# Keeping the first group's rows on the chip, and giving the prefill's operands memory that is released early

## The chip, the cores and the metric

The kernel runs on one core of one Trainium2 chip. The core has five engines with a queue each: TensorE (PE, matrix products), VectorE (DVE), ScalarE (ACT), GpSimd (POOL) and SyncE (SP, which here only issues DMAs). Each works through its instructions in the order of its program. Semaphores make an instruction wait for those of other engines. SBUF is the memory on the chip, PSUM the banks that take PE's results, and DRAM the memory behind the DMA queues. The metric is the time of one execution in microseconds on the device, as the median of several runs.

## What is computed

One layer of a hybrid backbone at width 1024, on 9 blocks of 128 tokens: block 0 is context, blocks 1 to 8 are latent tokens. Cut to what matters here:

```python
mods  = silu(c) @ w_ada + b_ada             # six rows: shift, scale, gate, twice
h     = rmsnorm(x) * (1 + scale1) + shift1
q, k, v, mq, mk, mv, mo, mgates = split(h @ w_in)
a     = attention(q, k, v)                  # 8 query heads, 2 key heads, 512 wide
m     = mlstm_bidir(mq, mk, mv, mgates)     # 4 heads, forward and backward scan, 512 wide
x     = x + gate1 * (concat(a, rmsnorm(m) * sigmoid(mo)) @ w_out)
h2    = rmsnorm(x) * (1 + scale2) + shift2
x     = x + gate2 * (swiglu(h2 @ w_gu) @ w_down)
y     = rmsnorm(x) * final_norm_w
```

The rows that the change is about are `x` after the out-projection, `x + gate1 * (...)`, which are added up in two halves: 512 input columns from attention, 512 from the mLSTM.

## The kernel before

**Tiling.** The 9 blocks form three groups of three (`CB` = 3). Products are made in float32 pieces split in two: a high part (`whi`, `mx`) rounded for PE and a low part (`wlo`, the second half of `mx`), so each product is three matmuls: high by high, high by low, low by high. For a weight piece, SP loads `raw` (128 x 1024 float32, 512 KB), ACT casts it to `whi` (L152), and DVE subtracts to make `wlo` (L137).

**Stages.** Up to about 455 us: norm, input projection, head projections, the scans of the mLSTM heads and the attention of group 0, woven together. Then the scan of the last head, woven with `attn_out_first`, which does the attention half of the out-projection for group 0 alone and leaves its rows in a tile `x1a`. Then `prefill`, about 492 to 560 us, on which the change bears. Then the FFN of the three groups, where PE does products of `aTh`/`aTl` and the gate, up and down weights to the end.

**The prefill.** For each block b = 0 to 8:

- `load_hm(b)`: the mLSTM rows, which the scan has stored to `hm_d` in DRAM, come back as `hmr`.
- `mix(b)`: four transposes on PE (L116), a cast on ACT (L1206) and a subtraction on DVE (L137) make the operand `mx`.
- `half(b, 0)` and `half(b, 1)`: one `out_block` each. It is 12 matmuls (L1163, L1164, L1165) into one of four PSUM banks. Then DVE multiplies by the gate row (L1124) and frees the bank, and POOL adds to the residual rows (L1125).
- for b below 3, `end(b)`: squares and their sum on ACT (L1325, `jk`), a reciprocal root in twelve small DVE steps (L127 to L133), and a block or two later `norm2`: `y` on ACT (L1341), transposes on PE, and the scaled and shifted operands of the FFN.

Blocks 0 and 1 are done together (first halves of both, then second halves), the others one by one. Attention of group 1 is woven in at 0.35 of a step per step: scores S on PE (L1055), their maximum on DVE (L1057), exponential on ACT (L1058, L1061), the low part on DVE (L1062), two DMA transposes (`phT`, `plT`, issued by SP), and the products with the values on PE (L1079, L1080).

The rows of group 0 take a way around: `attn_out_first` keeps `x1a` in memory that is released at its end, so POOL stores the three blocks to `x1a_d` in DRAM (L1297), and SP loads them again as `x` in the prefill (L1185). The second pair of out-projection pieces is issued behind the first two of these loads.

**What sets the order.** The code above is not the order on the engines. A scheduler simulates the program and chooses the next instruction of each engine from those that are ready in its model. Constraints (`issue_after`) and priorities (`hot`) in the code bend its choice. Tile pools decide on memory. A tile that takes the place of another waits until the old one's last reader is done, and a pool opened in place of closed ones inherits their waits. Before, `hmr` and `mx` lie in the pool `xp` on the right side, which takes the place of tiles of the scan that are in use to its end.

The last head's scan is the stage ahead: for each of the three groups POOL multiplies by the output gate (L905), ACT squares (L904, `jkh`), DVE makes the reciprocal root `ry` and POOL multiplies by it (L911). Then the group's rows are stored to `hm_d` (L914, L916): group 0 by SP, group 1 by ACT's queue, group 2 by POOL's queue.

## Time and profile before

| | |
|---|---|
| median of three runs | 1548.04 us (1547.23 to 1548.79) |
| the profiled execution, its own time | 1549.49 us |
| its span, first to last instruction | 1547.7 us |
| mean granted clock of TensorE | 0.981 |
| busy: PE, DVE, ACT, POOL | 1482.8, 1018.6, 772.2, 273.9 us |
| PE busy in 480 to 500, 500 to 510, 520 to 530 us | 13.65 of 20, 8.96 of 10, 3.96 of 10 us |

Busy times of different engines overlap. PE is busy for 96% of the span, so an engine's waits matter where PE waits for it. PE's granted clock is shown as a share of full speed: at 0.5 a matmul takes about twice the time and still counts as busy. The rows of a timeline give the start, the duration, the engine, the line, the operation with its tiles, and in brackets the idle time ahead of it with what ended it.

### The profile page before, as it was taken

What the parts mean: (1) busy time and instruction counts of PE and PEld (TensorE: products, weight loads), DVE (VectorE), ACT (ScalarE), POOL (GpSimd) and SP (SyncE); (2) the same over time, 40 slices, a digit from 0 to 9 for tenths busy, and PEclk for the clock granted to TensorE, in tenths of its full rate; (3) what the DMA queues carried; (4) which work ended last, traced back from release to release, by engine and by line L of the source; (5) the groups of instructions that cost most, each with busy time, mean ns of one, the idle gap of its engine ahead of it and who ended that gap; (6) DMA issues with size and microseconds to landing.
All of it is one profiled execution on the core that took longest, in us unless ns stands there. A gap on an engine that the chain in (4) does not pass through costs nothing.

```text
span 1547.7 us, 23430 instructions
## 1 busy us (share of the span) xinstructions
PE 1482.8 (96%) x8539; PEld 1248.4 (81%) x8539; DVE 1018.6 (66%) x2025; ACT 772.2 (50%) x1429; POOL 273.9 (18%) x356
## 2 busy tenths in 40 slices
PE   6899999999998899999999999999999999999997
PEld 3545567677766679899898989989898989999996
DVE  4878554838657865878646587887866484554554
ACT  4754465947654643555432445556642443323333
POOL 0112422333434352010110101000000101101110
PEclk9899999999998899999999999999999999999998
DMA  9664423522365766878644547878764545544441
GB/s 361 196 193 145 100 70 42 118 52 59 76 217 196 207 136 188 199 155 204 162 137 130 169 138 242 192 171 177 182 145 127 157 151 159 157 133 134 143 144 59
DMA packets 388057, 236.91 MB, mean 153 GB/s; under 512 B 170198, under 2 KB 347686, under 8 KB 387942
## 3 DMA queue, kind: packets, MB, share of 16 engines
q1 hardware_dynamic: 385438, 230.26, 54.4%
q10 hardware_dynamic: 2008, 3.39, 1.0%
q8 instruction: 67, 1.10, 0.3%
q0 software_dynamic: 496, 1.77, 0.3%
q14 instruction: 48, 0.39, 0.1%
HBM read 183.79 MB, written 13.26 MB: 127 GB/s over the span
## 4 chain that ended last, share of the span: by engine, by line
PE 83%; DVE 7%; ACT 4%; DMA 4%; issue 2%; POOL 1%; SPq 0%; ACTq 0%; DVEq 0%
PE mm L1363 12%; PE mm L1364 12%; PE mm L1362 12%; PE mm L1135 5%; PE mm L1136 5%; PE mm L1137 5%; PE S L1055 4%; PE wi L498 3%; PE wi L496 3%; PE wi L497 3%; PE mm L1165 2%; PE mm L1163 2%; PE mm L1164 2%; PE po L1079 2%; PE po L1080 2%
## 5 line engine op out<-in xcount | busy, mean ns | idle before, releaser
L152 ACT CAST whi<-raw 128x1024 fp32r<-128x1024 f32 (+1 forms) x216 | 221.8, 1027 | 395.8 <-PE mm L1363 148.3
L137 DVE TENSOR_TENSOR wlo<-raw,whi 128x1024 fp32r<-128x1024 f32 (+1 forms) x216 | 259.6, 1202 | 178.5 <-ACT whi L152 175.4
L1363 PE MATMUL mm<-aTl,whi 128*128 128x384 f32 x1056 | 355.9, 337 | 2.7 <-DVE aTl L137 2.7
L1364 PE MATMUL mm<-aTh,wlo 128*128 128x384 f32 x1056 | 354.3, 336 | 0.0
L1362 PE MATMUL mm<-aTh,whi 128*128 128x384 f32 x1056 | 353.3, 335 | 0.1
L137 POOL TENSOR_TENSOR hl<-tn,hl 128x384 fp32r<-128x384 f32 x66 | 84.3, 1277 | 846.1 <-ACT hl L1385 730.0
L1363 PEld LDWEIGHTS mm<-aTl,whi 128*128 128x128 f32 x1056 | 198.4, 188 | 3.9 <-DVE aTl L137 3.3
L1362 PEld LDWEIGHTS mm<-aTh,whi 128*128 128x128 f32 x1056 | 198.0, 188 | 1.0 <-ACT aTh L1356 0.4
L1364 PEld LDWEIGHTS mm<-aTh,wlo 128*128 128x128 f32 x1056 | 198.4, 188 | 0.1
L1136 PE MATMUL mm<-wlo,hl 128*128 128x512 f32 x372 | 145.5, 391 | 0.0
L1135 PE MATMUL mm<-whi,hl 128*128 128x512 f32 x372 | 144.3, 392 | 0.0
L1137 PE MATMUL mm<-whi,hl 128*128 128x512 f32 x372 | 142.8, 392 | 0.0
L1062 DVE SCALAR_TENSOR_TENSOR pl<-pr,st,ph 128x1152 f16<-128x1152 f32 (+1 forms) x72 | 95.3, 1323 | 35.6 <-ACT ph L1061 35.5
L1057 DVE TENSOR_REDUCE st<-S 128x1 f32<-128x1152 f32 (+1 forms) x72 | 88.8, 1233 | 16.5 <-PE S L1055 15.8
L1058 ACT ACTIVATE pr<-S,st 128x1152 f32<-128x1152 f32 (+1 forms) x72 | 81.4, 1130 | 29.1 <-DVE st L1057 28.4
L1061 ACT ACTIVATE ph<-pr,st 128x1152 f16<-128x1152 f32 (+1 forms) x72 | 83.8, 1164 | 23.3 <-DVE st L1060 11.0
L496 PE MATMUL wi<-headw,hT 128*128 128x384 f16 x288 | 93.9, 326 | 0.2 <-ACT th L775 0.2
L498 PE MATMUL wi<-headw,hT 128*128 128x384 f16 x288 | 93.9, 326 | 0.0
L497 PE MATMUL wi<-headw,hT 128*128 128x384 f16 x288 | 93.9, 326 | 0.0
L1124 DVE TENSOR_TENSOR t<-mm,gl 128x512 f32<-128x512 f32 x102 | 68.8, 685 | 32.4 <-PE mm L1137 8.4
L1055 PE MATMUL S<-kst,qT 128*128 128x384 f32 (+1 forms) x400 | 84.8, 344 | 1.0 <-ACT pr L1058 1.0
L1137 PEld LDWEIGHTS mm<-whi,hl 128*128 128x128 f32 x372 | 69.9, 188 | 14.4
(391 smaller groups left out, 2660.0 us busy)
## 6 DMA issues: line engine op xcount, KB each, us to landing
raw<-in_w_gu_dram SPq DMA_DIRECT2D x132, 512.0 KB
raw<-in_w_down_dram SPq DMA_DIRECT2D x60, 512.0 KB
a<-in_w_ada_dram SPq DMA_DIRECT2D x24, 512.0 KB
gl<-g_d SPq DMA_DIRECT2D x36, 256.0 KB
aw<-in_w_ada_dram SPq DMA_DIRECT2D x16, 512.0 KB
iraw<-in_w_in_dram SPq DMA_DIRECT2D x32, 256.0 KB
raw<-in_w_out_dram SPq DMA_DIRECT2D x12, 512.0 KB
x<-in_x_sample_dram SPq DMA_DIRECT2D x11, 512.0 KB
```

The source lines that it names most:

```text
L137: (dve if eng == "dve" else pool).tensor_tensor(out=out, in0=full, in1=hi, op=ALU.subtract)
L152: nc.scalar.copy(hi[:, :n], raw[:, :n])
L496: mm(ps[:, :n], ah, wh[:, k % 2, c0 : c0 + n], start=(k == 0), stop=False)
L497: mm(ps[:, :n], ah, wl[:, k % 2, c0 : c0 + n], start=False, stop=False)
L498: mm(ps[:, :n], al, wh[:, k % 2, c0 : c0 + n], start=False, stop=(k == KD - 1))
L1055: mm(S[:, n, 0:w], qT[:, h, :], kst[kv][:, t, c0 + n * w : c0 + (n + 1) * w], start=(t == 0), stop=(t == 1))
L1135: mm(ps, ah, wh[:, k % 2, :], start=(k == 0), stop=False)
L1136: mm(ps, ah, wl[:, k % 2, :], start=False, stop=False)
L1137: mm(ps, al, wh[:, k % 2, :], start=False, stop=(k == nk - 1))
L1362: mm(ps, wh[:, k, :], th[:, k, :], start=(k == 0), stop=False)
L1363: mm(ps, wh[:, k, :], tl[:, k, :], start=False, stop=False)
L1364: mm(ps, wl[:, k, :], th[:, k, :], start=False, stop=(k == KD - 1))
```

## The change

Four things are changed.

1. A new pool `rowp`, opened near the start, holds `x1a`. The rows of group 0 stay in it and go straight into the prefill as its residual rows. The three stores to `x1a_d` and the three loads from it are gone. The tag of that tile later holds the rows of group 2, and before it held a part of the input operand (`hT2`).
2. A new pool `xe` holds `hmr` and `mx` of the prefill, in memory that is released earlier than that of `xp`. A new pool `wl` takes one of the five buffer pairs for weight pieces.
3. Constraints on the order: the attention steps woven in are issued behind the loads of the gate rows, of the pieces and of `hmr` and behind the latest out-projection block; loads of later `hmr` behind the gate row; the second pair of pieces no longer behind the loads of group 0's rows.
4. The last head's store of group 1's mixed rows goes to POOL's queue and not to ACT's.

In the files the lines of the changed kernel lie five to six further down than before: L152 becomes L157, L904 becomes L909, L1055 becomes L1060, L1163 to L1165 become L1168 to L1170, L1206 becomes L1212.

On ACT, at the end of the last scan and the start of the prefill, there stands before (`jkh`: the scan's squares, `whi_6272` and `whi_6278`: the first two weight pieces, `mx_6303` and `mx_6313`: operands of b0 and b1):

```order
L904 ACTIVATE jkh_6171,ssh_5748<-hm_5747 128x128
L904 ACTIVATE jkh_6191,ssh_5748<-hm_5747 128x128
L901 ACTIVATE hm_5747<-nu_6194,dn_6205 128x128
L904 ACTIVATE jkh_6211,ssh_5748<-hm_5747 128x128
L152 CAST whi_6272<-raw_6271 128x1024
L916 DMA hm_d_76<-hm_5747 128x384
L152 CAST whi_6278<-raw_6277 128x1024
L1206 CAST mx_6303<-mm_6304 128x512
L1206 CAST mx_6313<-mm_6314 128x512
```

and now:

```order
L909 ACTIVATE jkh_6168,ssh_5748<-hm_5747 128x128
L157 CAST whi_6271<-raw_6270 128x1024
L1212 CAST mx_6300<-mm_6301 128x512
L909 ACTIVATE jkh_6188,ssh_5748<-hm_5747 128x128
L906 ACTIVATE hm_5747<-nu_6191,dn_6202 128x128
L1212 CAST mx_6310<-mm_6311 128x512
L157 CAST whi_6277<-raw_6276 128x1024
L909 ACTIVATE jkh_6208,ssh_5748<-hm_5747 128x128
```

The first weight piece and the operand of b0 moved ahead of two of the scan's squares, and the store is gone from this queue.

On PE, around the first scores of the prefill, there stands before (`mm_6351`: first half of b1, `mm_6368` and `mm_6404`: second halves of b0 and b1, `mm_6462`: transposes of b2):

```order
L1165 MATMUL mm_6351<-whi_6278,mx_6313 128x512
L1055 MATMUL S_6426<-kst_1028,qT_6341 128x384 x6
L1163 MATMUL mm_6368<-whi_6292,mx_6303 128x512
L1163 MATMUL mm_6404<-whi_6292,mx_6313 128x512
L116 MATMUL mm_6462<-ident,hmr_6311 128x128 x4
L1164 MATMUL mm_6368<-wlo_6293,mx_6303 128x512
```

and now (`mm_6400`: second half of b1, `mm_6458`: transposes of b2, `mm_6467` and `mm_6483`: the halves of b2):

```order
L1169 MATMUL mm_6400<-wlo_6296,mx_6310 128x512
L1170 MATMUL mm_6400<-whi_6295,mx_6310 128x512
L1060 MATMUL S_6422<-kst_1028,qT_6338 128x384 x6
L116 MATMUL mm_6458<-ident,hmr_6308 128x128 x4
L1168 MATMUL mm_6467<-whi_6271,mx_6457 128x512
L1169 MATMUL mm_6467<-wlo_6272,mx_6457 128x512
L1168 MATMUL mm_6483<-whi_6289,mx_6457 128x512
```

The scores moved behind all four blocks of b0 and b1, and the transposes of b2 from among these blocks to behind the scores.

On SP, behind the store of the last head's first rows, there stands before (`hmr`: mLSTM rows of b0 to b3, `gl` and `gx_all`: gate rows, `raw_7064`: the first gate/up piece of the FFN):

```order
L151 DMA raw_6271<-in_w_out_dram 128x2x512
L151 DMA raw_6277<-in_w_out_dram 128x2x512
L1178 DMA hmr_6267<-hm_d_75 128x512
L1178 DMA hmr_6269<-hm_d_75 128x512
...
L1185 DMA x_1234_6259<-x1a_d_79 128x1024
L1185 DMA x_1234_6259<-x1a_d_80 128x1024
L151 DMA raw_6291<-in_w_out_dram 128x2x512
L151 DMA raw_6297<-in_w_out_dram 128x2x512
...
L1185 DMA x_1234_6259<-x1a_d_81 128x1024
L1185 DMA x_1235_6260<-in_x_sample_dram 128x1024 x3
L151 DMA raw_7064<-in_w_gu_dram 128x8x128
```

and now:

```order
L1183 DMA hmr_6266<-hm_d_78 128x512
L1183 DMA hmr_6268<-hm_d_78 128x512
L156 DMA raw_6270<-in_w_out_dram 128x2x512
L156 DMA raw_6276<-in_w_out_dram 128x2x512
L156 DMA raw_6288<-in_w_out_dram 128x2x512
L156 DMA raw_6294<-in_w_out_dram 128x2x512
...
L1183 DMA hmr_6308<-hm_d_78 128x512
L1185 DMA hmr_6318<-hm_d_79 128x4x128
L1192 DMA x_1234_6262<-in_x_sample_dram 128x1024 x3
L156 DMA raw_7060<-in_w_gu_dram 128x8x128
```

The `hmr` loads of b0 and b1 moved ahead of the first pair of pieces, the second pair stands directly behind the first, and the three loads of group 0's rows are gone.

The diff, with lines that only rename left out:

```diff
+    rowp = ctx.enter_context(tc.tile_pool(name="rowp", bufs=1, reuse_waits="tile"))
...
-    x1a_d = [drp.tile([P, D], F32, name=f"x1a_d{i}") for i in range(CB)]
...
-        hi = own[0] if own else wp.tile([P, 1024], F32R, name=nm("whi"), tag="whi", bufs=5)
-        lo = own[1] if own else wp.tile([P, 1024], F32R, name=nm("wlo"), tag="wlo", bufs=5)
+        if not own:
+            loaded["n"] = (loaded["n"] + 1) % 5
+            at, bufs = (wp, 4) if loaded["n"] else (wl, 1)
+            own = [at.tile([P, 1024], F32R, name=nm(t), tag=t, bufs=bufs) for t in ("whi", "wlo")]
...
-                        ((None, nc.scalar.dma_start, pool.dma_start)[c] if alone else dma)(hm_d[c][:, h], hm[:, c * CB : (c + 1) * CB, :].rearrange("p b n -> p (b n)"))
+                        (pool.dma_start if alone else dma)(hm_d[c][:, h], hm[:, c * CB : (c + 1) * CB, :].rearrange("p b n -> p (b n)"))
...
-            hm = xp.tile([P, 512], F32, name=nm("hmr"), tag="hmr", bufs=2)
+            hm = xe.tile([P, 512], F32, name=nm("hmr"), tag="hmr", bufs=2)
...
-            if b < 2 * CB:
-                dma(x1s[b // CB][b % CB], x1a_d[b] if b < CB else xrow(b))
+            if CB <= b < 2 * CB:
+                dma(x1s[1][b % CB], xrow(b))
...
-        with tc.issue_after(dma(gx_all, g_d[0, 0:1, :].to_broadcast([P, D])).ins):
-            load_x1(0)
-            load_x1(1)
-            ws.append(out_pieces(1, 1))
+        gate = loaded["gate"] = dma(gx_all, g_d[0, 0:1, :].to_broadcast([P, D])).ins
+        ws.append(out_pieces(1, 1))
+        cur["gate"] = loaded["piece"]
...
-            t = xp.tile([P, NQ, P], F32R, name=nm("mx"), tag="mx", bufs=3)
+            t = xe.tile([P, NQ, P], F32R, name=nm("mx"), tag="mx", bufs=3)
...
-            hms.append(load_hm(b + 2))
+            with tc.issue_after(gate):
+                hms.append(load_hm(b + 2))
...
-        x1 = hTp.tile([P, CB, D], F32, name="x1a", tag="hT2")
+        x1 = rowp.tile([P, CB, D], F32, name="x1a", tag="b4")
...
-                    if n == 1:
-                        pool.dma_start(x1a_d[i], x1[:, i])
-
-        return out(), ada
+
+        return out(), ada, [x1[:, i] for i in range(CB)]
...
+    xe = ctx.enter_context(tc.tile_pool(name="xe", bufs=1, reuse_waits="tile"))
+    wl = ctx.enter_context(tc.tile_pool(name="wl", bufs=1, reuse_waits="tile"))
...
-    cur["x1"], nxt["x1"] = new_x1(0), new_x1(1)
+    cur["x1"], nxt["x1"] = x1_first, new_x1(1)
...
-            next(att, None)
+            with tc.issue_after(cur["gate"]), tc.issue_after(loaded["gate"]), tc.issue_after(loaded["hm"]), tc.issue_after(loaded["pe"]):
+                next(att, None)
...
-            for _ in range(4):
-                next(main)
+            with tc.issue_after(loaded["gate"]):
+                for _ in range(4):
+                    next(main)
```

More of the change, by code (lines that the diff above doesn't have):

```diff
@@ L147, in load_piece @@
         raw = raw or wp.tile([P, 1024], F32, name=nm("raw"), tag="raw", bufs=2)
[L148 to L149 removed]
+        if not own:
+            loaded["n"] = (loaded["n"] + 1) % 5
+            at, bufs = (wp, 4) if loaded["n"] else (wl, 1)
+            own = [at.tile([P, 1024], F32R, name=nm(t), tag=t, bufs=bufs) for t in ("whi", "wlo")]
+        hi, lo = own
         for part, ap_ in srcs:
[L151 removed]
+            loaded["piece"] = dma(part(view(raw)), ap_).ins
         nc.scalar.copy(hi[:, :n], raw[:, :n])
@@ L1164, in out_block @@
             mm(ps, th[:, k], wl[:, k % 2, :], start=False, stop=False)
-            mm(ps, tl[:, k], wh[:, k % 2, :], start=False, stop=(k == 3))
+            loaded["pe"] = mm(ps, tl[:, k], wh[:, k % 2, :], start=False, stop=(k == 3)).ins
         return ps
@@ L1475, in hybrid_step @@
     scan = head_mlstm(NH - 1, sts[NH - 1])
-    first, ada = attn_out_first(oT, done)
+    first, ada, x1_first = attn_out_first(oT, done)
     emit(att)
```

14 lines of the change are left out of this document (7 added, 7 removed).

## The prediction

> **What bounds the kernel now.** I read the span and clock first, then the busy totals, then windows cut at the places where the granted clock changes, then the timelines of TensorE (PE), ScalarE (ACT), VectorE (DVE), GpSimd (POOL) and SyncE (SP) between 480 and 560 us. The core's row, the busy row of the page, and the windows (busy time of each engine, then the granted clock, the DMA share and GB/s):
>
> ```profile
> core 0: 1547.7 us, clock 0.981
> PE 1482.8 (96%) x8539; PEld 1248.4 (81%) x8539; DVE 1018.6 (66%) x2025; ACT 772.2 (50%) x1429; POOL 273.9 (18%) x356
> 494.70:505.25 10.55, 5.66 (x15) 4.27 (x16) 8.09 (x23) 4.92 (x9) 2.67 (x4) 0.51 0.76 257
> 505.25:525.50 20.25, 18.07 (x85) 14.87 (x83) 15.41 (x27) 10.75 (x14) 9.97 (x6) 1.00 0.93 289
> 525.50:535.75 10.25, 6.39 (x29) 5.08 (x30) 9.33 (x38) 7.33 (x13) 3.11 (x2) 0.50 0.49 109
> 535.75:549.10 13.35, 11.17 (x65) 9.56 (x63) 11.77 (x23) 9.28 (x16) 8.12 (x5) 1.00 0.51 108
> 549.10:552.90 3.80, 3.80 (x12) 3.01 (x11) 1.18 (x4) 2.63 (x4) 2.19 (x2) 0.55 0.07 14
> 560.00:600.00 40.00, 40.00 (x216) 34.12 (x215) 22.29 (x31) 14.75 (x19) 13.75 (x10) 1.00 0.75 200
> ```
>
> PE is busy for 1482.8 of 1547.7 us, and from 560 us on it has no hole: there nothing but less PE work helps, and the change takes none away. Everything it can win lies in the prefill, 490 to 560 us. There time is lost in two ways. PE waits, and after a wait it runs at half clock (0.50 to 0.55 in three windows). The waits of PE, from its timeline (start, duration, line, operation, in brackets the idle time before and what ended it):
>
> ```profile
> 498.54 0.80 PE L1163 MATMUL mm<-whi,mx 128*128 128x512 f32 x1 [5.15 <-ACT mx L1206]
> 501.66 0.80 PE L1165 MATMUL mm<-whi,mx 128*128 128x512 f32 x1 [1.04 <-DVE mx L137]
> ...
> 526.19 0.40 PE L1079 MATMUL po<-phT,vs 128*128 128x256 f16 x1 [2.87 <-DMA phT<-ph]
> 529.75 1.97 PE L116 MATMUL mm<-ident,y 128*128 128x128 f32 x8 [3.17 <-ACT y L1341]
> 548.51 0.28 PE L1079 MATMUL po<-phT,vs 128*128 128x256 f16 x1 [2.18 <-DMA phT<-ph]
> ```
>
> Together 14.4 us. Half clock costs half of PE's busy time in a slow window: 5.66/2 + 6.39/2 + 3.80/2 = 7.9 us. So at most some 22 us (1.4%) can be had, and the question is how much of it comes back elsewhere.
>
> **Step A, the first wait.** The first out-projection block needs the weights `whi` and the mixing operand `mx`, both made by ACT, which works in order:
>
> ```profile
> 492.82 0.19 ACT L904 ACTIVATION_READ_ACCUMULATOR jkh<-hm 128x1 f32 x1
> ...
> 495.84 1.03 ACT L152 CAST whi<-raw 128x1024 fp32r<-128x1024 f32 x1
> 497.91 1.07 ACT L1206 CAST mx<-mm 128x512 fp32r<-128x512 f32 x2
> 507.45 1.05 ACT L152 CAST whi<-raw 128x1024 fp32r<-128x1024 f32 x1 [3.92 <-DMA raw<-in_w_out_dram]
> ```
>
> In the new order the first `whi` and the first `mx` stand directly behind the `jkh` that ends at 493.0, ahead of the last two: 493.05 + 1.03 + 0.54 (half of the 1.07) = 494.6 instead of 498.54. The second and third products need DVE:
>
> ```profile
> 495.41 0.15 DVE L133 SCALAR_TENSOR_TENSOR ry<-rt,ry 128x3 f32<-128x3 f32 x1
> 497.49 1.23 DVE L137 TENSOR_TENSOR wlo<-raw,whi 128x1024 fp32r<-128x1024 f32 x1
> 500.93 1.28 DVE L137 TENSOR_TENSOR mx<-mm,mx 128x512 fp32r<-128x512 f32 x2
> ```
>
> The last `ry` step of the second group's rows still goes ahead, at about 495.1 (one `hm` of 0.35 us that stood before it moves behind), so `wlo` runs 495.2 to 496.4 and the low part of `mx` (0.64) to 497.05. From there PE does the four blocks of b0 and b1 without a stop, since the head's scores S (L1055) now stand behind all four and not between them:
>
> ```profile
> 503.96 0.63 PE L1164 MATMUL mm<-wlo,mx 128*128 128x512 f32 x1
> 504.39 0.63 PE L1165 MATMUL mm<-whi,mx 128*128 128x512 f32 x1
> 508.35 1.21 PE L1055 MATMUL S<-kst,qT 128*128 128x384 f32 x6
> 509.40 0.63 PE L1163 MATMUL mm<-whi,mx 128*128 128x512 f32 x2
> 510.02 0.63 PE L116 MATMUL mm<-ident,hmr 128*128 128x128 f32 x4
> 510.43 0.49 PE L1164 MATMUL mm<-wlo,mx 128*128 128x512 f32 x1
> 515.79 0.39 PE L1165 MATMUL mm<-whi,mx 128*128 128x512 f32 x1
> 516.02 1.21 PE L1055 MATMUL S<-kst,qT 128*128 128x384 f32 x6
> ```
>
> A matmul goes by every 0.43 us at half clock (503.96 to 504.39) and every 0.23 at full (515.79 to 516.02). The edges of the clock in the windows above lie about 3.4 us or multiples of it apart (10.25 = 3 x 3.42, 13.35 = 4 x 3.34, 3.80), and a slow phase ended after a stretch in which PE was busy throughout. Counted from 494.7, such a stretch is 498.1 to 501.5. So of the 46 matmuls left at 497.05, 10 go at 0.43 (4.45 us, to 501.5) and 36 at 0.23 (8.3), with 0.6 for the four transposes of `qr` and 1.05 for S (508.35 to 509.40): done at 511.45. Before, that work was done at 516.02 less what stood in it of b2 (four transposes 0.41, two matmuls 0.46): 515.15. Step A: **3.7 us gained**. Its condition is that the weight pieces are there. Before, SP asked for the second pair at 499.64:
>
> ```profile
> 499.64 1.91 SPq L151 DMA_DIRECT2D raw<-in_w_out_dram  x2
> 503.83 3.94 SPq L1185 DMA_DIRECT2D x<-in_x_sample_dram  x3
> 510.40 0.38 SPq L151 DMA_DIRECT2D raw<-in_w_gu_dram  x1
> ```
>
> Now SP asks for the first pair behind the two `hmr` loads (about 487.4), and for the third and fourth when their buffers are free, at 496.4 and about 499.2. The piece asked for at 499.64 was there at 507.45, 7.8 us later, but where the DMA share was 0.93, where 1.5 MB of the first group's rows were loaded too. These loads are gone, so I take 5 us: 492.4, 501.4, 504.2, in time for PE (needed at 493.05, 503.8 and 505.2). The ends: 7.8 us costs about 4 (a rival below); nothing late costs none, and a clock that comes back one stretch earlier gives 1.7 more.
>
> **Step B, what is late next.** Behind S, PE needs a free PSUM bank for b2's transposes. All four are held by the four blocks, and DVE empties them only behind the maximum of S:
>
> ```profile
> 505.82 0.69 DVE L1124 TENSOR_TENSOR t<-mm,gx_all 128x512 f32<-128x512 f32 x1 [1.56 <-DMA qr<-q_d]
> 510.29 1.35 DVE L1057 TENSOR_REDUCE st<-S 128x1 f32<-128x1152 f32 x1
> 511.68 1.23 ACT L1058 ACTIVATE pr<-S,st 128x1152 f32<-128x1152 f32 x1 [0.40 <-DVE st L1057]
> 506.60 1.29 POOL L1125 TENSOR_TENSOR x<-x,t 128x512 f32<-128x512 f32 x1 [3.62 <-DVE t L1124]
> 515.92 2.40 POOL L1125 TENSOR_TENSOR x<-x,t 128x512 f32<-128x512 f32 x1 [4.40 <-DVE t L1124]
> 518.35 1.06 ACT L1325 ACTIVATE jk<-x 128x1024 bf16<-128x1024 f32 x1 [3.37 <-POOL x L1125]
> ```
>
> First new wait: 1.35 + 0.69 = 2.04 us, to 513.5. Second: b2's `mx` stands behind the exponential (from 512.8, 1.4 for it and its read, then 0.54) and is ready at 514.75, PE's transposes at 513.9: 0.85. These two leave a 3.4 us stretch mostly idle, so I count half clock for the next: 1.7. Then 24 matmuls (5.5) and S (1.05): 523.0. Third: the normalized row `y` of b0 needs three POOL adds (1.29 to 2.40 each, I take 1.95) from 513.5, so 519.4, the squares (1.25), twelve small DVE steps (0.15 each at 495.41, with the gaps 2.3), and on ACT the squares of b1 and the cast of the first gate/up piece ahead of it: PE starts the transposes about 524.3 and waits 1.3. Fourth: b3's `mx` now stands behind b2's squares, which wait for POOL, which waits for DVE's `wlo` of that same piece: cast done 523.5, then 1.23, 0.69, 1.95, 1.06 and 0.54 make 529.0, against PE at about 525.9; 3.0 waited, and 1.7 of half clock after it. Together 2.04 + 0.85 + 1.7 + 1.3 + 3.0 + 1.7 = 10.6. Before, the same work lost 2.87 + 3.17 and 3.2 of half clock, 9.2: PV (L1079) no longer stands ahead of the transposes, and `y` comes at 524 and not 529. Step B: **1.4 us lost**. Its ends are 4.4 better (no half clock, adds at 1.29) and 4.7 worse (adds at 2.40, the gate/up piece 3 us late).
>
> A rule bears on the half clock. The Trainium skill, TensorE: Matmul & The Clock Gate, section "What's actually happening", says that the clock falls to half after at least one idle window of about 3.4 us and returns after a busy one, the windows running free. The returns and the spacing of the edges agree. The fall does not: 2.18 us idle before 548.51 was enough for 0.55 in 549.1 to 552.9. By the rule to the letter none of the new waits of step B would slow the clock.
>
> **Step C, the last wait.** Before, 2.18 us and half of 3.80 were lost at 546 to 553: 4.1. PV now follows b3's blocks, so its transposed operand has the time of 24 matmuls more to arrive. But S of each head still follows the exponential of another closely, and ACT and DVE carry the same work, so a wait may take its place. Between 0 and 4.1 I take the middle: **2.0 us gained**.
>
> **What costs nothing.** The three stores of the first group's rows on POOL and the store of the second group's mixed rows, which moves from ACT's queue to POOL's:
>
> ```profile
> 502.38 0.60 POOL L916 DMA_DIRECT2D hm_d<-hm  x1 [0.40 <-POOL hm L911]
> x1a_d<-x1a POOLq DMA_DIRECT2D x3, 512.0 KB, 5.5
> ...
> hm_d<-hm POOLq DMA_DIRECT2D x1, 192.0 KB, 6.9
> ```
>
> POOL is busy for a quarter to a half of this time. The added store costs it 0.6 us where it waits for DVE anyway. Its rows are read by b3's load, which stands on SP just ahead of the x rows; 6.9 us after about 497 is early enough there. The store of the third group's rows is the one with something behind it: SP waits for it before the x rows and the gate/up pieces. Its rows are ready later than before, since DVE's last `ry` steps now stand behind the third and fourth `wlo` and both `qT`: store at about 507.5 instead of 502.38, landed 514.4. The three x rows took SP 3.94 us to issue, one piece 0.38; I take 2.6 for the three, so the gate/up piece is asked for at 517 instead of 510.4 and there at 522, just when ACT comes to it.
>
> **Sum.** 3.7 - 1.4 + 2.0 = 4.3 us. The profiled execution took 1549.49 us (span 1547.7 and 1.8 around it) and would take 1545.2; the median of the runs is 1548.04, so the forecast is 1543.7.
>
> **Rivals.**
> - More is won. The second and third group of waits are covered: no half clock in B (3.4) and all of C (2.1 more): 9.8 us, 1538.2. For it: POOL is free of three software stores, so its adds start at once. Against it: DVE is 76 and 91% busy in the two windows there (15.41 of 20.25, 9.33 of 10.25), and every new wait is behind DVE or ACT.
> - Only the clock stays up, as the skill's rule to the letter has it. By the rows, as a mechanism here: if waits of 2.04 + 0.85 and 3.0 leave the clock alone, 3.4 are saved, 1540.3. Against it stands the row at 548.51.
> - The change does not do what it says: each weight piece takes 7.8 us to land. The first then comes at 495.2, 2.1 late, and the fourth about 2 late: 4 of the 4.3 are gone, 1547.7, no change. For it: the first pair is asked for only 5.6 us ahead of its use. Against it: six transfers of 512 KB, 3 MB, are gone.
> - Slower, by the store of the third group's rows. Whatever it lands later than 514.4 delays x rows, gate/up piece, `y` of b0 and b3's `mx` one for one, since all stand in a row on SP and ACT. It turns the sign at 4.3 us and passes 0.2% at 7.4, that is a landing at 522, 14 us after its issue, or less with one more slow-clock stretch (1.7 each). At 8 us: 1551.7. For it: SP is in order and 6.9 us was measured once only. Against it: DMA is less loaded.
>
> **Numbers.** Forecast (gain 3.1 to 6.5) 0.38; more won 0.14; clock alone 0.10; pieces late 0.22; slower 0.16. 0.2% is 3.1 us, about what a measurement of this kernel can tell from no change; so faster 0.62, same 0.22, slower 0.16. The range reaches to both outer rivals without their tails: 1537 to 1551.
>
> **What would show it.** Right: PE's 5.15 us wait split into short ones that end by 497.1; four blocks in a row before the first S, which starts near 510.4; a 2 us wait of the b2 transposes for DVE L1124; no wait for phT; `y` near 524; step by step the same program from 560 on, 4 us earlier. Wrong: `whi` waiting for its piece after 493, an x row or gate/up piece issued after 520, slow-clock windows longer than 14 us in sum, or POOL adds above 2.4 us.

## The result: no change

| | kernel before | changed kernel |
|---|---|---|
| median of 14 runs each | 1548.48 us | 1549.12 us |
| lowest and highest | 1543.80 to 1553.94 us | 1546.03 to 1551.88 us |
| ratio, 95% interval | | 1.0001 (0.9989 to 1.0013) |
| profiled execution, span | 1549.49, 1547.7 us | 1550.36, 1548.6 us |

The forecast was 4.3 us faster. The interval leaves room for 1.7 us of gain and 2.0 us of loss.

The busy row of the profile's page of the changed kernel shows nearly the same work as before:

```profile
PE 1483.4 (96%) x8539; PEld 1246.9 (81%) x8539; DVE 1020.2 (66%) x2025; ACT 772.1 (50%) x1429; POOL 268.2 (17%) x354
```

Windows of the changed kernel, cut where its granted clock changes (busy time of PE, PEld, DVE, ACT, POOL, then the clock, the DMA share and GB/s):

```profile
495.35:498.75 3.40, 3.07 (x7) 2.23 (x8) 3.37 (x7) 1.73 (x5) 3.17 (x4) 0.50 0.47 154
498.75:515.85 17.10, 13.21 (x61) 10.16 (x60) 9.27 (x22) 5.98 (x8) 3.79 (x4) 1.00 0.71 247
515.85:519.25 3.40, 3.40 (x10) 2.63 (x9) 3.00 (x4) 1.48 (x3) 1.50 (x3) 0.50 1.09 337
519.25:529.50 10.25, 6.38 (x33) 4.68 (x31) 9.66 (x31) 5.87 (x9) 4.67 (x3) 1.00 0.69 162
529.50:536.30 6.80, 6.14 (x15) 4.79 (x16) 4.83 (x20) 4.38 (x9) 0.63 (x1) 0.50 0.23 45
536.30:560.00 23.70, 21.16 (x119) 17.79 (x118) 18.87 (x34) 13.73 (x23) 15.54 (x11) 1.00 0.48 108
560.00:600.00 40.00, 38.11 (x212) 32.95 (x210) 24.10 (x32) 15.53 (x20) 11.63 (x9) 1.00 0.76 185
```

The three slow stretches of before (10.55, 10.25 and 3.80 us) have become 3.40, 3.40 and 6.80. So the time at half clock fell from 24.6 to 13.6 us. By half of PE's busy time, the loss is (3.07 + 3.40 + 6.14)/2 = 6.3 us where it was 7.9. The last row is new: from 560 to 600 us PE was busy for all of 40.00 us before, and now for 38.11.

PE's waits of the changed kernel, from its timeline:

```profile
494.82 0.50 PE L1168 MATMUL mm<-whi,mx 128*128 128x512 f32 x1 [1.09 <-ACT mx L1212]
495.68 0.80 PE L1169 MATMUL mm<-wlo,mx 128*128 128x512 f32 x1 [0.36 <-DVE wlo L137]
...
504.16 0.39 PE L1170 MATMUL mm<-whi,mx 128*128 128x512 f32 x1
504.95 0.50 PE L1168 MATMUL mm<-whi,mx 128*128 128x512 f32 x1 [0.41 <-ACT whi L157]
506.21 0.50 PE L1169 MATMUL mm<-wlo,mx 128*128 128x512 f32 x1 [0.76 <-DVE wlo L137]
...
510.18 1.21 PE L1060 MATMUL S<-kst,qT 128*128 128x384 f32 x6
513.44 0.66 PE L116 MATMUL mm<-ident,hmr 128*128 128x128 f32 x4 [2.05 <-DVE t L1129]
514.77 0.51 PE L1168 MATMUL mm<-whi,mx 128*128 128x512 f32 x1 [0.68 <-ACT mx L1212]
528.63 0.50 PE L1168 MATMUL mm<-whi,mx 128*128 128x512 f32 x1 [3.71 <-ACT mx L1212]
530.16 0.80 PE L1170 MATMUL mm<-whi,mx 128*128 128x512 f32 x1 [0.79 <-DVE mx L137]
542.30 1.32 PE L1060 MATMUL S<-kst,qT 128*128 128x384 f32 x6 [1.63 <-ACT pr L1063]
555.81 0.50 PE L1170 MATMUL mm<-whi,mx 128*128 128x512 f32 x1 [0.91 <-DVE mx L137]
570.29 0.50 PE L1168 MATMUL mm<-whi,mx 128*128 128x512 f32 x1 [0.68 <-ACT mx L1212]
596.90 0.27 PE L1084 MATMUL po<-phT,vs 128*128 128x256 f16 x1 [0.59 <-DMA phT<-ph]
599.03 0.27 PE L1085 MATMUL po<-plT,vs 128*128 128x256 f16 x1 [0.62 <-DMA plT<-pl]
```

The waits add up to 14.3 us, where the five long ones of before made 14.4. The wait of 5.15 us at the first block is gone, and so are those for `phT`, for `y` and at 548 us. In their place stand a free bank for b2 (2.05), b3's operand (3.71 + 0.79), S (1.63) and a tail of three short ones in the FFN.

To see where a lead is won and lost, the traces are compared at equal work. From the last product of the out-projection's attention half (485.56 us before, 485.81 after) every matmul of the prefill and the FFN counts with its spacing at full clock (0.2275 us for a product of the prefill, 0.109 for a transpose or PV, 0.175 for S, 0.173 for a product of the FFN); the scan's last matmuls do not count. The table shows by how many us a trace is ahead of the one before when PE has done so much work:

| PE work done since, us | 1 | 8 | 12 | 20 | 28 | 40 | 56 | 104 |
|---|---|---|---|---|---|---|---|---|
| place | first product | second halves | first S | b2 | b3 | b5 | end of prefill | FFN |
| changed kernel | 4.0 | 5.5 | 4.3 | -0.6 | 0.5 | 2.5 | 0.8 | -0.7 |
| kernel before, profiled again (e4) | -0.2 | -1.1 | -1.1 | -1.1 | 0.0 | 1.3 | 1.3 | 1.3 |

The second line of numbers is what two profiles of one kernel differ by, so a single number of this table is good to about 1.3 us. The lead of 4 to 5 us is there up to the first S. It is gone at b2. What comes back up to b5 (2.5) is lost again by the end of the prefill and at the start of the FFN.

### The profile page after: what moved, and what is told of

The parts are those of the page before. It is cut to its first block, busy times and chain, and to the rows that moved or that the text cites. A ratio compares the mean times of both kernels' runs of the same rounds, so it can differ in the third digit from the quotient of the medians.

```text
span 1548.6 us, 23402 instructions
## 1 busy us (share of the span) xinstructions
PE 1483.4 (96%) x8539; PEld 1246.9 (81%) x8539; DVE 1020.2 (66%) x2025; ACT 772.1 (50%) x1429; POOL 268.2 (17%) x354
## 4 chain that ended last, share of the span: by engine, by line
PE 58%; DVE 2%; DMA 1%; ACT 1%; issue 0%; SPq 0%; ACTq 0%
PE mm L1368 12%; PE mm L1369 12%; PE mm L1367 12%; PE mm L1140 5%; PE mm L1141 5%; PE mm L1142 5%; PE S L1060 3%; PE po L1085 1%; PE po L1084 1%; DMA raw<-in_w_gu_dram 1%; PE mm L1170 1%; PE mm L1169 1%; PE mm L1168 1%; DVE fl L1356 1%; DVE t L1129 0%; DVE x L1130 0%
## 5 line engine op out<-in xcount | busy, mean ns | idle before, releaser
L157 ACT CAST whi<-raw 128x1024 fp32r<-128x1024 f32 (+1 forms) x216 | 221.8, 1027 | 384.5 <-PE mm L1368 150.5
L1060 PE MATMUL S<-kst,qT 128*128 128x384 f32 (+1 forms) x400 | 84.6, 344 | 2.4 <-ACT pr L1063 2.4
L1142 PEld LDWEIGHTS mm<-whi,hl 128*128 128x128 f32 x372 | 69.9, 188 | 14.4
```

Of the source, the lines that this page charges most:

```text
L157: nc.scalar.copy(hi[:, :n], raw[:, :n])
L1060: mm(S[:, n, 0:w], qT[:, h, :], kst[kv][:, t, c0 + n * w : c0 + (n + 1) * w], start=(t == 0), stop=(t == 1))
L1142: mm(ps, al, wh[:, k % 2, :], start=False, stop=(k == nk - 1))
```

## The experiments

In each batch the kernels ran on one chip beside the kernel before (median 1549.03 us in the first, 1549.58 in the second, 1549.77 in the third).

| run | kernel | median, us | ratio (95% interval) |
|---|---|---|---|
| e1_no_pe_rule | changed, attention not held behind PE's blocks | 1549.35 | 1.0002 (0.9991 to 1.0012) |
| e2_old_memory | changed, operands in the old memory | 1550.89 | 1.0015 (1.0003 to 1.0026) |
| e3_rows_only | before, with the kept rows alone | 1544.88 | 0.9971 (0.9960 to 0.9982) |
| e4_before_again | before, unchanged | 1549.43 | 1.0001 (0.9991 to 1.0011) |
| e5_att_earlier | changed, attention woven in at 0.42 | 1552.98 | 1.0023 (1.0011 to 1.0035) |
| e6_rows_att_later | e3, attention at 0.30 | 1546.31 | 0.9977 (0.9967 to 0.9988) |
| e7_rows_memory_store | e3, with the memory and the store of the change | 1547.60 | 0.9987 (0.9973 to 1.0000) |
| e8_rows_att_earlier | e3, attention at 0.42 | 1547.09 | 0.9985 (0.9970 to 0.9999) |
| e9_no_order_rules | changed, without rules on attention and later loads | 1552.44 | 1.0019 (1.0011 to 1.0028) |
| e10_scores_between | changed, first S between the second halves | 1550.10 | 1.0003 (0.9990 to 1.0016) |
| e11_rows_memory | e3, with the memory of the change | 1546.14 | 0.9977 (0.9964 to 0.9990) |
| e12_rows_store_sync | e3, the second group's store on SP | 1549.32 | 1.0000 (0.9989 to 1.0012) |

**e1_no_pe_rule.** The rule that holds a woven-in attention step behind the latest out-projection block is taken out:

```diff
-            with tc.issue_after(cur["gate"]), tc.issue_after(loaded["gate"]), tc.issue_after(loaded["hm"]), tc.issue_after(loaded["pe"]):
+            with tc.issue_after(cur["gate"]), tc.issue_after(loaded["gate"]), tc.issue_after(loaded["hm"]):
```

> The changed kernel without one of its four rules for the attention steps: they no longer have to issue behind the latest out-projection block. In its order the first scores S stand again behind the first halves of b0 and b1, and PV of the first head inside b2's blocks. Theory (the gain at the first wait, some 4 us, is real and is given back because the rule puts the attention behind the blocks): no wait of b2's transposes for DVE L1124 of 2 us, no wait of 3.7 us for b3's mx, no wait for phT near 597 to 599 us; 2 to 5 us faster than the changed kernel, 1544 to 1547. Rival (the gain is eaten by what SP and POOL bring late, the x rows and the gate/up piece behind the store of the third group): y of b0 and b3's mx come as late as now, 1548 to 1550.

Measured: no change against before (1.0002). The lead was 5.3 us at work 12 and -3.7 at work 20. PE's timeline of this kernel shows where:

```profile
514.50 2.29 PE L1060 MATMUL S<-kst,qT 128*128 128x384 f32 x6 [4.46 <-ACT pr L1063]
...
532.26 2.29 PE L1060 MATMUL S<-kst,qT 128*128 128x384 f32 x6 [3.18 <-ACT pr L1063]
```

The bank wait is gone, and S waits 4.46 us for the exponential of the scores before it. Without the rule the time is the same, so the theory that put the lost gain down to this rule alone falls.

**e2_old_memory.** `hmr` and `mx` go back to the pool `xp`:

```diff
-            hm = xe.tile([P, 512], F32, name=nm("hmr"), tag="hmr", bufs=2)
+            hm = xp.tile([P, 512], F32, name=nm("hmr"), tag="hmr", bufs=2)
...
-            t = xe.tile([P, NQ, P], F32R, name=nm("mx"), tag="mx", bufs=3)
+            t = xp.tile([P, NQ, P], F32R, name=nm("mx"), tag="mx", bufs=3)
...
```

> The changed kernel with hmr and mx of the prefill back in the old memory (pool xp); all else as changed, and PE's order is the same. Theory (the early first product comes from this memory): ACT makes mx of b0 only behind the scan's squares and behind all four casts of weight pieces, the first product comes at 498 to 503 us and not at 494.8, and the kernel is 4 to 8 us slower than the changed one, 1553 to 1557. Rival (the memory does nothing, the order and the kept rows do): the first product at 495 to 496, 1548 to 1550.

Measured: 1550.89 us, 1.0015. That is less than the theory's 4 to 8 us over the changed kernel, and near the rival's time. The first product comes at 503.10, as late as the theory had it, but what PE waits for is not ACT. It is the load of `hmr`, and the loads of `hmr` stand on SP behind all four weight pieces, where they stood ahead of them in the changed kernel:

```profile
481.50 13.78 SPq L156 DMA_DIRECT2D raw<-in_w_out_dram  x4
495.38 0.89 SPq L1183 DMA_DIRECT2D hmr<-hm_d  x2
```

```profile
501.34 1.94 PE L116 MATMUL mm<-ident,hmr 128*128 128x128 f32 x8 [10.60 <-DMA hmr<-hm_d]
```

At the first product this kernel is 5.6 us behind the kernel before and 9.6 behind the changed one. At work 28 it is 0.7 behind, at work 104 0.6 behind, the changed kernel 0.7. In these two profiles 9.6 us at the front are worth nothing at the end.

By the names of the tiles, PE's order is that of the changed kernel throughout, but DVE's is not: the multiplications that empty the first banks stand ahead of the maximum of the first scores, and behind it PE's transposes of b2 wait for nothing.

```profile
508.11 0.69 DVE L1129 TENSOR_TENSOR t<-mm,gx_all 128x512 f32<-128x512 f32 x1 [3.49 <-PE mm L1170]
517.79 1.36 DVE L1062 TENSOR_REDUCE st<-S 128x1 f32<-128x1152 f32 x1 [0.30 <-PE S L1060]
```

In the medians the old memory is 1.8 us slower (1550.89 against 1549.12), but these come from two batches, and the intervals of the two ratios overlap.

**e3_rows_only and e4_before_again.** e3 is the kernel before with the first part of the change and nothing else:

```diff
+    rowp = ctx.enter_context(tc.tile_pool(name="rowp", bufs=1, reuse_waits="tile"))
...
-            if b < 2 * CB:
-                dma(x1s[b // CB][b % CB], x1a_d[b] if b < CB else xrow(b))
+            if CB <= b < 2 * CB:
+                dma(x1s[1][b % CB], xrow(b))
...
-            load_x1(0)
-            load_x1(1)
...
-                    if n == 1:
-                        pool.dma_start(x1a_d[i], x1[:, i])
...
```

> The kernel before with one part of the change alone: the rows of group 0 stay on the chip, no stores, no loads. Memory of hmr and mx, the rules for the attention and the queue of the store as before. Theory: the second pair of weight pieces is not behind the row loads any more and the first pair comes earlier on ACT, so the first wait falls from 5.2 to about 3 us and the last two waits for phT stay: 1 to 3 us faster than before, 1545 to 1547. Rival (the rows' way around was hidden): 1548 to 1549.

> The kernel before once more, for the spread of the prefill's waits from one profile to another. If the waits belong to the order of the instructions, the same five waits of PE above 0.5 us stand between 495 and 560 us, each within 0.5 us, in sum 14 to 15 us; if they hang on chance in the DMAs, they differ by more. Time 1547 to 1550.

Measured: e3 is 0.29% faster (1544.88 us, 4.2 us below the median of before in its batch), the best of all kernels here. The repeat of before gave 1.0001, and its five waits came back, each within 0.43 us of the first profile and 14.05 us in sum, so they belong to the order of the instructions; a sixth of 0.54 stands among them. SP's queue, the first cast and low part, and PE's waits in e3:

```profile
490.51 0.80 SPq L1155 DMA_DIRECT2D gl<-g_d  x2
491.65 0.32 SPq L1191 DMA_DIRECT2D gx_all<-g_d  x1
493.99 2.18 SPq L151 DMA_DIRECT2D raw<-in_w_out_dram  x2
```

```profile
491.33 1.04 ACT L152 CAST whi<-raw 128x1024 fp32r<-128x1024 f32 x1
492.74 1.22 DVE L137 TENSOR_TENSOR wlo<-raw,whi 128x1024 fp32r<-128x1024 f32 x1
```

```profile
498.46 0.79 PE L1163 MATMUL mm<-whi,mx 128*128 128x512 f32 x1 [5.16 <-ACT mx L1204]
...
524.85 1.27 PE L116 MATMUL mm<-ident,y 128*128 128x128 f32 x8 [2.37 <-ACT y L1337]
527.51 0.28 PE L1079 MATMUL po<-phT,vs 128*128 128x256 f16 x1 [0.95 <-DMA phT<-ph]
```

The first wait is still whole (5.16 us), where the theory expected about 3. The time came out just below its range. In the kernel before, SP stood still for the rows' stores until just ahead of 498.75:

```profile
SPq L1185 <- DMA x1a_d<-x1a: 6.5, 1, 6.5
```

That wait is gone, and SP issues the second pair of pieces at 493.99 and not at 499.64. The stores were not the only hold: a piece needs a buffer, and the first one came free before only when DVE had made the low part, at 498.72 (the row at 497.49 in the prediction). In e3 it is free at 493.96, because ACT casts the first piece at 491.33 instead of 495.84. So the scheduler has put the instructions of PE, ACT and DVE in another order too (PE's differs at 135 of 8539 places), and what the stores and loads do by themselves is not separated from that. ACT casts the second pair from 502.35 (507.45 before), the first gate/up piece from 513.02 (520.61), and `y` comes at 524.09 (528.98). The waits for `phT` and `y` shrink from 2.87 + 3.17 to 0.95 + 2.37. At equal work the trace is ahead by 1.5 us at work 8, 3.2 at 28 and 4.3 from work 56 to the end. So the removal of the loads and stores that the prediction costed at nothing, with the order that the scheduler makes without them, is the part that pays.

**e5_att_earlier.** The tail in the FFN comes from attention steps that the change has put later. Here they are woven in faster:

```diff
-        due += 0.35
+        due += 0.42
```

> The changed kernel with the attention of group 1 woven in at 0.42 of a step per prefill step instead of 0.35; its rules stay. The first product stays at 494.8 us. Theory (in the changed order the attention ends too late, and what PE is ahead is lost again where the FFN waits for the last operands phT and plT near 597 to 599 us): PE reaches the end of prefill with attention done, these two waits go, 2 to 4 us faster than the changed kernel, 1545 to 1547. Rival (the loss is made at b2 and b3, by the bank wait and by b3's mx behind POOL's adds, whatever the attention does): these waits stay near 2 and 3.7 us and the time at 1548 to 1550.

Measured: 1.0023, slower. The bank wait grows, and new ones stand behind it:

```profile
518.01 0.66 PE L116 MATMUL mm<-ident,hmr 128*128 128x128 f32 x4 [3.85 <-DVE t L1129]
...
535.98 0.80 PE L1170 MATMUL mm<-whi,mx 128*128 128x512 f32 x1 [2.21 <-DVE mx L137]
...
613.10 0.28 PE L1084 MATMUL po<-phT,vs 128*128 128x256 f16 x1 [1.58 <-DMA phT<-ph]
616.82 0.27 PE L1085 MATMUL po<-plT,vs 128*128 128x256 f16 x1 [0.82 <-DMA plT<-pl]
```

The waits for `phT` and `plT` do not go; they come later and are longer. At work 56 this trace stood at -0.2, and behind it 3.8 us more are lost. So a larger number does not mend the tail, and whether only the tail was in the way this run cannot say.

**e6_rows_att_later and e8_rows_att_earlier.** The same number is changed in e3, to 0.30 and to 0.42.

> Rows of group 0 kept and nothing else (the fastest so far, 1544.9 against 1549.0 of before), with the attention woven in at 0.30 instead of 0.35. PE's order gets like that of the changed kernel: the scores behind more of the second halves, PV of the first head behind b3's blocks. Theory (later attention costs): 2 to 4 us slower than with 0.35, 1547 to 1549, with waits for phT or plT at the start of the FFN. Rival (the order of the attention matters little, the casts and row loads do): within 1 us of 1545.

> Rows kept and nothing else, with the attention at 0.42 instead of 0.35. Theory: the attention is not late at 0.35 here, so nothing is won: 1544 to 1546. Rival (earlier is always better): 1542 to 1543.5.

Measured: 0.9977 and 0.9985, both still faster than before, by their medians 1.4 and 2.2 us slower than e3. e3 ran in another batch and the intervals of the three ratios overlap, so neither loss is sure. e6 lost less than its theory expected, and e8 lies above the 1544 to 1546 of its theory. The gain of the kept rows does not hang on this number.

**e7_rows_memory_store and e11_rows_memory.** e11 adds to e3 only the pool `xe` for `hmr` and `mx`; e7 adds the store of the second group's rows on POOL's queue as well:

```diff
-                        ((None, nc.scalar.dma_start, pool.dma_start)[c] if alone else dma)(hm_d[c][:, h], hm[:, c * CB : (c + 1) * CB, :].rearrange("p b n -> p (b n)"))
+                        (pool.dma_start if alone else dma)(hm_d[c][:, h], hm[:, c * CB : (c + 1) * CB, :].rearrange("p b n -> p (b n)"))
...
-            hm = xp.tile([P, 512], F32, name=nm("hmr"), tag="hmr", bufs=2)
+            hm = xe.tile([P, 512], F32, name=nm("hmr"), tag="hmr", bufs=2)
...
-            t = xp.tile([P, NQ, P], F32R, name=nm("mx"), tag="mx", bufs=3)
+            t = xe.tile([P, NQ, P], F32R, name=nm("mx"), tag="mx", bufs=3)
...
```

> Rows kept, and of the change also the early memory for hmr and mx and the store of group 1's rows on POOL's queue; none of the rules on the order. PE's order is that of the kept rows alone. ACT no longer has the store, which waits for POOL, ahead of mx: first product near 497 instead of 498.5. Theory (a lead at the front is not passed on, the chain of adds, squares, root and y behind it is): y of b0 stays near 524 and the time within 1 us of the kept rows alone, 1544 to 1546. Rival (a lead at the front is passed on): 1 to 2 us faster, 1543 to 1544.

> The kept rows, and the prefill's operands in the memory released early, with PE's order as with the kept rows alone. Theory (a lead at the first block isn't passed on to the end): the first product comes up to 1 us earlier, the end like the kept rows alone, 1544 to 1546.5. Rival (the memory itself costs, since what is put into its place waits for the scan): 1547 to 1549, with a new wait of the x rows' loads.

Measured: 0.9987 and 0.9977. In both the order on PE, ACT, DVE and POOL is that of e3. In e11 the first product still waits 5.21 us for `mx`; in e7 it waits 4.07, and this 1.1 us does not reach the end. At work 104 they are 3.4 (e7) and 4.8 us (e11) ahead. The median of e7, 1547.60, lies above the 1544 to 1546 of its theory, but its interval overlaps that of e3. The memory neither wins nor costs anything that these runs can tell. What it makes possible, an earlier first product, comes only with the change's other order.

**e9_no_order_rules.** Here the changed kernel keeps rows, memory, early pieces and store, and loses the rules for attention steps, later `hmr` loads and the first steps of the FFN:

```diff
-            with tc.issue_after(cur["gate"]), tc.issue_after(loaded["gate"]), tc.issue_after(loaded["hm"]), tc.issue_after(loaded["pe"]):
-                next(att, None)
+            next(att, None)
...
-            with tc.issue_after(gate):
-                hms.append(load_hm(b + 2))
+            hms.append(load_hm(b + 2))
...
-            with tc.issue_after(loaded["gate"]):
-                for _ in range(4):
-                    next(main)
+            for _ in range(4):
+                next(main)
```

> The change without its rules for the order: attention steps and later hmr loads are free to stand where the scheduler puts them; rows, memory, the second pair of pieces and the store stay as changed. Theory (the order is what gives the kept rows' gain back): S and PV stand among the blocks again as before, the bank wait of 2.05 us before b2's transposes goes, and the whole comes out like the kernel with the kept rows alone, 1544.5 to 1547, ahead of the kernel before by 2 to 4 us at the end. Rival (it is the memory and the early pieces that cost, through the casts on ACT and the wlo on DVE standing ahead of the maximum): it stays at 1548 to 1550.

Measured: 1552.44 us, 1.0019, slower; 1544.5 to 1547 was expected. The theory falls: without the rules the kernel is not faster, and by the medians 3.3 us slower than the changed one. PE, SP and DVE of this kernel:

```profile
522.11 1.12 PE L116 MATMUL mm<-ident,hmr 128*128 128x128 f32 x4 [4.76 <-DVE t L1129]
```

```profile
496.45 2.96 SPq L156 DMA_DIRECT2D raw<-in_w_out_dram  x2
...
514.88 0.49 SPq L1198 DMA_DIRECT2D gx_all<-g_d  x1
```

```profile
518.11 1.35 DVE L1062 TENSOR_REDUCE st<-S 128x1 f32<-128x1152 f32 x1
521.36 0.69 DVE L1129 TENSOR_TENSOR t<-mm,gx_all 128x512 f32<-128x512 f32 x1 [1.90 <-DMA gx_all<-g_d]
```

The lead reaches 7.2 us at work 8 and is -7.8 at work 20. The gate row `gx_all` stands on SP behind the weight pieces and behind two DMA transposes. It is asked for at 514.88, and DVE waits 1.90 us for it before it empties the first bank at 521.36. The rest of the lateness is DVE's order: three maxima of scores (the last at 518.11) stand ahead of that multiplication.

**e10_scores_between.** In the changed kernel the first S may stand between the second halves of b0 and b1:

```diff
+            first = loaded["pe"]
             half(b, 1)
+            loaded["pe"] = first
```

> The change with the first scores S let in between the second halves of b0 and b1 and not behind them. Theory (the wait for a PSUM bank behind the maximum of S is what costs): the 2.05 us wait and the half clock behind it (1.7) go, 1545 to 1547. Rival (the chain of DVE, POOL and ACT to the row y and b3's operand sets the pace, whatever stands before it): the time saved at 513 us is waited for again by 537 us, and it stays at 1548 to 1550.

Measured: 1.0003, near the time of the rival. The first S moved on PE, from 510.18 to 505.89. But the bank wait does not go, it grows to 3.02 us, and b3's `mx` (3.39) and an S (3.12) wait behind it. On DVE the first multiplication stands behind the maximum and, here, behind the low part of the exponential too, and starts at 513.51. So an earlier first S on PE does not by itself free the banks.

**e12_rows_store_sync.** e3 with the second group's store on SP:

```diff
-                        ((None, nc.scalar.dma_start, pool.dma_start)[c] if alone else dma)(hm_d[c][:, h], hm[:, c * CB : (c + 1) * CB, :].rearrange("p b n -> p (b n)"))
+                        ((None, dma, pool.dma_start)[c] if alone else dma)(hm_d[c][:, h], hm[:, c * CB : (c + 1) * CB, :].rearrange("p b n -> p (b n)"))
```

> The kept rows, and the store of the second group's mixed rows on SP and not on ACT's queue, with PE's order as with the kept rows alone. Theory (before the first mx ACT stands behind the issue of this store, which waits for POOL): mx comes 1 to 2 us earlier and the first wait of 5.16 us falls to 3.2 to 4.2; of this 0 to 2 reach the end, 1543 to 1545. Rival (SP now stands still behind the store's rows and asks for the pieces later): the second pair is late, 1546 to 1548.

Measured: 1.0000; the whole gain of e3 is gone, with the order on PE, ACT, DVE and POOL unchanged. The theory falls. The rival had it that SP stands still, but put the price too low: not only the pieces but the `hmr` loads and the gate rows stand behind the store on SP, which waits there 14.0 us for POOL:

```profile
497.17 0.34 SPq L916 DMA_DIRECT2D hm_d<-hm  x1
497.62 0.86 SPq L1178 DMA_DIRECT2D hmr<-hm_d  x2
...
499.53 0.38 SPq L1191 DMA_DIRECT2D gx_all<-g_d  x1
```

```profile
500.43 1.94 PE L116 MATMUL mm<-ident,hmr 128*128 128x128 f32 x8 [9.06 <-DMA hmr<-hm_d]
```

In e3 the `hmr` loads were issued at 486.04 and `gx_all` at 491.65. At equal work the first product is 4.0 us later than in e3, and the end 5.8 us; by the medians it is 4.4. So in this order of work a delay at the front does reach the end, in full.

**The runs side by side.** In the changed kernel SP and DVE look like this:

```profile
487.15 11.47 SPq L156 DMA_DIRECT2D raw<-in_w_out_dram  x4
498.71 0.92 SPq L1160 DMA_DIRECT2D gl<-g_d  x2
499.68 1.09 SPq L1198 DMA_DIRECT2D gx_all<-g_d  x1
```

```profile
511.43 1.36 DVE L1062 TENSOR_REDUCE st<-S 128x1 f32<-128x1152 f32 x1 [4.28 <-PE S L1060]
512.70 0.68 DVE L1129 TENSOR_TENSOR t<-mm,gx_all 128x512 f32<-128x512 f32 x1
```

SP issues four pieces in a row. For the third and fourth it stands still until a buffer is free; with these waits the four issues take 11.47 us, and the gate rows stand behind them. `gx_all` is asked for 13.9 us behind the last product of the attention half; before it was 6.2. The first bank is emptied at 512.70, where it was 505.82 before and 504.11 in e3.

But DVE does not wait for the gate row here: no instruction of this trace waits for `gx_all`, whose semaphore is complete at 506.9. DVE idles for 4.28 us, from 507.2 to 511.4, for the first S, because in its order the maximum of S stands ahead of the multiplications that empty the banks. Over 14 profiles, counted from the last product of the attention half:

| kernels | `gx_all` asked for, us | first bank emptied, us | on DVE ahead of the first maximum | ratio |
|---|---|---|---|---|
| before, e4 | 6.2, 6.4 | 20.3, 20.9 | yes | 1.0000, 1.0001 |
| e3, e6, e7, e8, e11 | 6.0 to 6.3 | 18.7 to 19.7 | yes | 0.9971 to 0.9987 |
| e12, e2 | 14.4, 12.7 | 22.7, 23.6 | yes | 1.0000, 1.0015 |
| changed, e1, e10, e5 | 13.9 to 15.6 | 26.9 to 30.6 | no | 1.0001 to 1.0023 |
| e9 | 28.3 | 34.7 | no | 1.0019 |

All kernels that keep the rows and ask for the gate rows early come out below the kernel before (0.9971 to 0.9987, though the interval of e7 reaches 1.0000); none that asks for them late does. That is what the runs show. It does not make the late gate rows the cause. In e12 and e2 the loads of `hmr` are late with them, and PE waits 9.06 and 10.60 us for these. In the changed kernel, e1, e5 and e10 nothing waits for the gate rows, and what holds the first bank is DVE's order. e2 has PE's order of the changed kernel and DVE's the other way round: there the wait of b2's transposes is gone, and from work 12 to 28 it wins 2.7 us on the kernel before, where the changed kernel loses 3.8. It starts 9.6 us later, though, so that this is no clean comparison.

That the scheduler puts the maximum first because the second pair of pieces makes the gate rows late in its model would join all this, but no run shows it. Not tried were the changed kernel with the second pair behind the gate rows, the same with the multiplications ahead of the maximum on DVE, and e3 with the early pair alone.

## Why the prediction failed

The time lies in the range, which was wide enough to hold no change and some loss as well; the likeliest case, 4.3 us faster, did not come. By its steps:

- **Step A (3.7 gained): right.** 4.3 at the first S. The first product came at 494.82 (494.6 was predicted), the first S at 510.18 (510.4). The clock came back one stretch earlier than reckoned. What ate this again was the third and fourth piece, which were said to be in time: PE waited 0.41 and 0.76 for them.
- **Step B (1.4 lost): mechanism right, size wrong.** At work 28 the lead is 0.5, so 3.8 us were lost. The bank wait was 2.05 (2.04 predicted), `mx` of b2 0.68 (0.85), the half clock behind them 3.40/2 (1.7). `y` came at 522.44 and PE did not wait for it (1.3). At b3 it was worse: 3.71 + 0.79 (3.0), and two slow stretches, 6.14/2 = 3.1 (1.7). Together 12.0 where 10.6 was reckoned. The other 1.0 of the 2.4 that were missing are not pinned down; a difference of this size lies within what two profiles of one kernel differ by.
- **Step C (2.0 gained): right, as far as the table tells.** From work 28 to 40 the lead rises from 0.5 to 2.5. As was said, a wait for S took the place of the one removed (1.63 us).
- **A term that was missing.** "Step by step the same program from 560 on" was wrong. Attention steps had moved out of the prefill, and their end lies in the FFN: 0.68 + 0.59 + 0.62 = 1.89 us of waits, all that PE lacks in the window 560 to 600 (40.00 - 38.11). The lead fell from 2.5 at work 40 to -0.7 at the end; these waits and the one at 555.81 (0.91) are 2.8 of the 3.2. In e3 nothing is lost from work 40 on (4.3 and 4.3).
- **"What costs nothing": the largest mistake.** The rows' stores and loads were costed as busy time of POOL and found hidden. They did not lie in PE's way by their time, but by their place: SP stood 6.5 us for the stores, with the second pair of pieces behind them. Taking them away alone, with the order that the scheduler then makes, is worth 4.2 us (e3). The prediction saw that these loads were gone and used it only for how fast the pieces land.
- **What turned that around: located, but not explained to the end.** The prediction had it right that DVE empties the banks only behind the maximum of S, and priced this as a wait of PE (2.04, and 2.05 came). It did not price the 4.28 us for which DVE itself idles at 507. Between 519 and 530 us DVE is busy for 9.66 of 10.25, so it can hardly make them up; this is an argument, and no run tests it. The sum also had SP ask for the third and fourth piece "when their buffers are free" and did not count the gate rows, which stand behind them on SP and are asked for 7.7 us later. In the order rows of SP ahead of the prediction they are among those left out. Whether they led to DVE's order stays open.

Of the rivals, "pieces late" gave the right time for another reason: the pieces cost 1.2 us, not 4. "Slower, by the store" did not happen: the third group's store was issued at 508.54 and the x rows at 510.79, 2.3 us later, where the prediction took 6.9 for the landing. "Only the clock stays up" is refuted: after the waits of 2.05 + 0.68 us a stretch at 0.50 followed.

## What to carry to other kernels

An engine that issues DMAs in order is a resource like any other. When a load or a store moves ahead, ask what stands behind it, above all if it has to wait itself: in e12 a store that waits on SP took back the whole gain of e3. A lead at the front need not reach the end (in the profiles e2 starts 9.6 us behind the changed kernel and ends level with it), so look at what the other engines do with it, and in which order: here DVE stood idle while the results that it could have taken were there. Where a change has several parts, run each alone: here one part was worth 4 us and the whole nothing. And where a scheduler makes the order, compare the order of every engine before a run is called a test of one part.

## What was not expected of the hardware

- **A stop of PE costs more than its idle time.** Without a stop a product follows the one ahead every 0.23 us (515.79 to 516.02 in the prediction's rows), though it is shown as lasting 0.39. From the product at 504.16 above to the one behind the stop, at 504.95, it takes 0.79 us, 0.41 of it idle: 0.15 more than the two together. To the next, at 506.21, it takes 1.26, 0.76 idle: 0.27 more. That is about what a product overlaps with its successor in the stream, and a stop loses it. The ends of matmuls are modelled in the profile, so how much of this counts as idle is the profile's choice.
- **Small waits are enough for the slow clock.** In the 3.40 us ahead of 515.80 PE is busy for 1.68, and 3.40 us at 0.50 followed, as after the 2.18 us of waiting in the row at 548.51 of before (the window is below). The Trainium skill, TensorE: Matmul & The Clock Gate, section "What's actually happening", asks for at least one idle window of about 3.4 us; the length of the slow stretches (3.40 and 6.80) agrees with it, the fall again does not.

```profile
512.40:515.80 3.40, 1.68 (x9) 1.28 (x10) 3.01 (x7) 2.77 (x4) 2.32 (x2) 1.00 0.98 377
```

- **How fast a store on POOL's queue lands varies.** The profile's page of before gives 6.9 us for the one store of `hm_d`. In the changed kernel the median of two is half of that, and in e12 it is 9.1:

```profile
hm_d<-hm POOLq DMA_DIRECT2D x2, 192.0 KB, 3.6
```
